# The swapped key copy of the rotary step, moved from VectorE to ScalarE in a two-layer decoder trunk

## The chip, the cores and the metric

The kernel runs on one core of one Trainium2 chip. Its metric is the device time of one execution in microseconds (us). An execution that the hardware profiler took shows what each engine did. The engines are named as the profile names them: PE (TensorE matmuls), PEld (its weight loads), DVE (VectorE), ACT (ScalarE), POOL (GpSimd), SP (the queue that issues the DMAs, SPq in its rows).

## The reference

Two layers of a decoder over 1024 tokens of width 1024. Layer 0 mixes tokens by dilated sliding-window attention in three groups, layer 1 by sliding-window attention with grouped keys and sinks; each mixer is gated, projected, normalised and followed by a gated embedding. The change touches the step between the rotary embedding and the scores.

```python
def apply_rope(t, cos, sin):
    tf = t.astype(jnp.float32)
    half = HEAD_DIM // 2
    t1, t2 = tf[..., :half], tf[..., half:]
    c, s = cos[None, :, None, :], sin[None, :, None, :]
    return jnp.concatenate([t1 * c - t2 * s, t2 * c + t1 * s], axis=-1).astype(t.dtype)
...
def mixer_a(x, w_in, w_out, cos, sin):
    h = x @ w_in
    for gi, (window, dil) in enumerate(A_GROUPS):
        base = 3 * gi * A_WIDTH
        q, k, v = split_cols(h[..., base:base + 3 * A_WIDTH], [A_WIDTH] * 3)
        q = apply_rope(q.reshape(B_, S, A_HEADS, HEAD_DIM), cos, sin)
        k = apply_rope(k.reshape(B_, S, A_HEADS, HEAD_DIM), cos, sin)
        o, lse = banded_attention(strided(q)[:, :, :, None, :], strided(k), strided(v), window // dil)
```

## The kernel before, in words

Every product is made of float16 pieces: a number is split into a high half and a low half (what the high half leaves over), and a product is three matmuls, high by high, high by low, low by high (`lin`, lines 270 to 272; 24 matmuls of 128x512 for a tile of 128 tokens by 512 columns). Tokens stand in 8 tiles of 128.

Layer 0 (`layer_a`, line 622) goes through 2 pairs of head groups, 3 dilations and, in each, a block of values (8 tiles, `v_out`) and two blocks of queries and keys (8 tiles each, 4 query heads and 4 key heads in a tile). So there are 96 query and key tiles. The product of such a tile goes through `rope_out` (line 335): two products with the tables on DVE (lines 345 and 348), their sum on POOL (line 349), the high half on ACT (line 355), the low half on POOL (line 356), the swapped key copy (line 359) and a DMA that transposes the result into `qk` (line 360). A head's row in `hl` is its 64 high halves and then its 64 low halves; the swapped copy of a key has the low halves first, so that two matmuls (line 383) make the full score.

An attention unit is one tile of 4 heads. It runs as `scores` (line 370): the score matmuls on PE (line 383), mask and maximum on DVE (line 387), the bias, four exponentials and the high half of the result on ACT (lines 391, 393, 397), the low half on POOL or DVE (line 399), and a transposing DMA into `pT` (line 402); two units later the value matmuls on PE read `pT` (lines 414 to 416) and ACT copies their result out (line 694). There are 96 units in layer 0 and 32 in layer 1. Score and value matmuls are interleaved with the matmuls of `lin`, and weights of later blocks are prepared meanwhile: maxima on DVE (line 108), a scale over PE (line 235, which waits for line 228 on DVE), and the split on ACT and DVE (lines 131 and 132). At the end of layer 0 the three dilations are merged (`merge`, lines 740 to 768, on DVE, ACT and POOL), and their result is loaded again, transposed to `ogT` and projected.

In layer 1 (`layer_b`, line 787) only the 8 tiles of keys (2 heads, line 805) have the swapped copy; its query tiles have none (`nk` is 0).

What sets the order of the work: each engine has one queue that runs strictly in its order, SP's queue of DMA issues too. The order is not the one of the source: the framework's scheduler arranges the instructions of all engines from its own estimate of their durations (line 1140), so that an instruction put on another engine moves others as well.

Of the kernel before, what the change touches and what calls it, by code (L numbers as in the profile page):

```python
# [14 lines left out]
AF = mybir.ActivationFunctionType  # L15
# [123 lines left out]
class Trunk:  # L139
# [195 lines left out]
    def rope_out(self, ps, nq, nk, n, dst):  # L335

        nc, w = self.nc, self.work
        nh = nq + nk  # L340
        t1 = w.tile([P, 512], F32, tag="t1", name="t1")
        t2 = w.tile([P, 512], F32, tag="t2", name="t2")
        pv = ps.rearrange("p (h c) -> p h c", c=32)
        cos = self.cos[:, n, :].unsqueeze(1).to_broadcast([P, 2 * nh, 32])
        nc.vector.tensor_mul(t1[:, :nh * HD].rearrange("p (h c) -> p h c", c=32), pv, cos)  # L345
        pb = ps.rearrange("p (h b c) -> p h b c", b=2, c=32)[:, :, ::-1, :]
        sin = self.sin[:, n].unsqueeze(1).to_broadcast([P, nh, 2, 32])
        nc.vector.tensor_mul(t2[:, :nh * HD].rearrange("p (h b c) -> p h b c", b=2, c=32), pb, sin)  # L348
        nc.gpsimd.tensor_add(t1[:, :nh * HD], t1[:, :nh * HD], t2[:, :nh * HD])  # L349
        nb = nh + nk  # L350
        hl = w.tile([P, 12, P], F16, tag="hl", name="hl", bufs=3)
        rv = t1[:, :nh * HD].rearrange("p (h c) -> p h c", c=HD)

        def parts():
            nc.scalar.activation(hl[:, :nh, 0:HD], rv, AF.Copy)  # L355
            nc.gpsimd.tensor_sub(hl[:, :nh, HD:P], rv, hl[:, :nh, 0:HD])  # L356
            if nk:
                src, to = (hl[:, a:b, :].rearrange("p h (w c) -> p h w c", w=2) for a, b in ((nq, nh), (nh, nb)))
                nc.vector.tensor_copy(to, src[:, :, ::-1, :])  # L359
            nc.sync.dma_start(dst, hl[:, :nb, :].rearrange("p b c -> p (b c)"), transpose=True)  # L360

        self.ends.append(parts)
# [781 lines left out]
```

## Time and profile before

| | us |
|---|---|
| median of 3 runs | 1685.56 (1683.73 to 1686.35) |
| the profiled execution | 1685.33 |
| its span in the profile | 1683.5 |
| PE busy | 1595.0 (95%) |
| DVE busy | 1130.6 (67%) |
| ACT busy | 871.7 (52%) |
| POOL busy | 677.5 (40%) |

A line of a group gives line, engine, operation, tiles, shape and count, then busy time and the mean duration of one in ns, then the idle time of the engine just ahead of it and what ended it. A line of a timeline gives start and duration in us, and in brackets the idle time ahead with what ended it. In a wait, "A <- B: x, n, y" is x us in all, n times, y the longest.

### The profile page before, as it was taken

To read this page: it belongs to the slowest core of one execution; us is meant where nothing else is said; L and a number is where in the kernel's file an instruction comes from. 1 tells how busy PE (TensorE), PEld (TensorE's weight loads), DVE (VectorE), ACT (ScalarE), POOL (GpSimd) and SP (SyncE) were. 2 spreads that over 40 slices of the span, in tenths; PEclk is the share of its full clock that TensorE was granted. 3 is DMA by queue.
4 is the path that set the end of the run, shared out by engine and by line. 5 is a ranking of instruction groups with operands and counts; after the bars stand their busy time and mean duration, and the time that the engine had idled before them with its cause. 6 is when DMAs were issued, how large, how long until landed. Compare 5 with 4: busy or idle time off the path is not lost. (4 is left out here: it accounts for less than half of the span.)

```text
span 1683.5 us, 29019 instructions
## 1 busy us (share of the span) xinstructions
PE 1595.0 (95%) x10579; PEld 881.5 (52%) x10579; DVE 1130.6 (67%) x2721; ACT 871.7 (52%) x1946; POOL 677.5 (40%) x481
## 2 busy tenths in 40 slices
PE   9898999999999889999999988898999998999999
PEld 3455566654555445766545544344455555544444
DVE  6767556665667776566656696887447898778631
ACT  4525564564755355655647662633232888853321
POOL 0215423532554565234325654443323552225441
PEclk9999999999999999999999999899999999999999
DMA  9617855773678668557647986989965798987963
GB/s 361 242 60 160 171 145 123 174 159 108 140 160 219 190 137 176 151 132 163 155 114 157 193 224 208 316 242 276 233 179 133 139 207 176 182 292 219 248 209 113
DMA packets 543791, 311.02 MB, mean 185 GB/s; under 512 B 473120, under 2 KB 494240, under 8 KB 543392
## 3 DMA queue, kind: packets, MB, share of 16 engines
q1 hardware_dynamic: 543648, 309.16, 74.1%
q8 instruction: 83, 1.36, 0.3%
q14 instruction: 60, 0.49, 0.1%
HBM read 137.78 MB, written 54.92 MB: 114 GB/s over the span
## 5 line engine op out<-in xcount | busy, mean ns | idle before, releaser
L270 PE MATMUL lin<-whl,xhl 128*128 128x512 f16 x1280 | 491.2, 384 | 0.0
L271 PE MATMUL lin<-whl,xhl 128*128 128x512 f16 x1280 | 490.3, 383 | 0.0
L272 PE MATMUL lin<-whl,xhl 128*128 128x512 f16 x1280 | 489.9, 383 | 0.0
L349 POOL TENSOR_TENSOR t<-t,t 128x512 f32<-128x512 f32 (+1 forms) x120 | 152.4, 1270 | 265.2 <-DVE t L348 233.0
L399 POOL TENSOR_TENSOR phl<-sm,phl 128x1024 f16<-128x1024 f32 (+1 forms) x88 | 156.9, 1783 | 245.4 <-ACT phl L397 217.8
L108 DVE TENSOR_REDUCE wpm<-wraw 128x1 f32<-128x1024 f32 (+1 forms) x132 | 157.1, 1198 | 92.6 <-DMA wraw<-in_wa_dram 48.2
L272 PEld LDWEIGHTS <-xhl 128*128 128x128 f16 x1280 | 149.5, 117 | 128.0 <-issue 5.3
L270 PEld LDWEIGHTS <-xhl 128*128 128x128 f16 x1280 | 149.5, 117 | 120.1 <-issue 5.4
L271 PEld LDWEIGHTS <-xhl 128*128 128x128 f16 x1280 | 150.4, 117 | 118.1 <-issue 5.3
L393 ACT ACTIVATE sm<-sm,st,cs 128x128 f32<-128x128 f32 (+1 forms) x384 | 203.6, 532 | 3.8 <-ACT mw L752 0.3
L356 POOL TENSOR_TENSOR hl<-t,hl 128x512 f16<-128x512 f32 (+1 forms) x120 | 145.4, 1212 | 124.6 <-ACT hl L355 124.6
L387 DVE CUSTOM_DVE_ANT_0 sm<-s,tab 128x256 f32<-128x256 f32 (+1 forms) x512 | 156.9, 359 | 33.6 <-PE s L383 31.9
L355 ACT ACTIVATE hl<-t 128x512 f16<-128x512 f32 (+1 forms) x120 | 72.3, 603 | 190.6 <-POOL t L349 181.5
L132 DVE SCALAR_TENSOR_TENSOR whl<-wraw,s,whl 128x1024 f16<-128x1024 f32 (+1 forms) x116 | 161.4, 1445 | 3.1 <-ACT whl L131 3.0
L131 ACT ACTIVATE whl<-wraw,s 128x1024 f16<-128x1024 f32 (+1 forms) x116 | 121.9, 1123 | 26.6 <-PE lin L272 10.2
L270 PE MATMUL lin<-whl,x2T 128*128 128x512 f16 (+1 forms) x320 | 115.5, 361 | 0.0
L271 PE MATMUL lin<-whl,x2T 128*128 128x512 f16 (+1 forms) x320 | 115.2, 360 | 0.0
L272 PE MATMUL lin<-whl,x2T 128*128 128x512 f16 (+1 forms) x320 | 115.2, 360 | 0.0
L397 ACT ACTIVATE phl<-sm 128x1024 f16<-128x1024 f32 (+1 forms) x128 | 110.7, 865 | 3.6 <-DMA pT<-phl 1.6
L345 DVE TENSOR_TENSOR t<-lin,rope 128x512 f32<-128x512 f32 (+1 forms) x120 | 78.9, 658 | 47.2 <-PE lin L272 46.9
L359 DVE COPY hl<-hl 128x512 f16<-128x512 f16 (+1 forms) x104 | 55.7, 535 | 74.7 <-POOL hl L356 74.6
L414 PEld LDWEIGHTS <-pT 128*128 128x128 f16 x800 | 72.8, 99 | 46.4 <-DMA pT<-phl 44.0
(190 smaller groups left out, 2913.7 us busy)
## 6 DMA issues: line engine op xcount, KB each, us to landing
wraw<-in_wa_dram SPq DMA_DIRECT2D x56, 512.0 KB, 5.1
scr<-st SPq DMA_DIRECT2D x96, 132.0 KB, 2.4
gt<-scr SPq DMA_DIRECT2D x48, 264.0 KB, 3.5
wraw<-in_wav_dram SPq DMA_DIRECT2D x24, 512.0 KB, 5.6
prh<-pro SPq DMA_DIRECT2D x32, 256.0 KB, 4.4
wraw<-in_wg_dram SPq DMA_DIRECT2D x16, 512.0 KB, 7.7
wraw<-in_wb_dram SPq DMA_DIRECT2D x16, 512.0 KB, 6.7
xg<-y SPq DMA_DIRECT2D x16, 512.0 KB, 3.8
```

The source lines that it names most:

```text
L108: k.nc.vector.tensor_reduce(pm[:, c:c + 1], self.raw[:, c * q:(c + 1) * q], axis=AX.X, op=ALU.max, apply_absolute_value=True)
L131: nc.scalar.activation(hl[:, 0, sl], self.raw[:, sl], AF.Copy, scale=self.s)
L132: nc.vector.scalar_tensor_tensor(hl[:, 1, sl], self.raw[:, sl], self.s, hl[:, 0, sl], op0=ALU.mult, op1=ALU.subtract)
L270: mm(ps, xh(kt), wh, start=(kt == 0), stop=False)
L271: mm(ps, xh(kt), wl, start=False, stop=False)
L272: mm(ps, xl(kt), wh, start=False, stop=(kt == NK - 1))
L349: nc.gpsimd.tensor_add(t1[:, :nh * HD], t1[:, :nh * HD], t2[:, :nh * HD])
L356: nc.gpsimd.tensor_sub(hl[:, :nh, HD:P], rv, hl[:, :nh, 0:HD])
L387: nc.vector.tensor_tensor_reduce(sm[:, h, :nk], ps[:, i, :nk], mask, 1.0, -3e38, ALU.add, ALU.max, mx[:, h:h + 1])
L393: nc.scalar.activation(sm[:, h, :nk], sm[:, h, :nk], AF.Exp, bias=nbias[:, h:h + 1], scale=cs, accum_out=sums[:, h:h + 1])
L397: nc.scalar.activation(hl[:, 0], sm[:, :, :nk], AF.Copy)
L399: eng.tensor_sub(hl[:, 1], sm[:, :, :nk], hl[:, 0])
```

## The change

The copy is issued on ACT as an activation that copies, with the same source and destination.

```diff
             if nk:
                 src, to = (hl[:, a:b, :].rearrange("p h (w c) -> p h w c", w=2) for a, b in ((nq, nh), (nh, nb)))
-                nc.vector.tensor_copy(to, src[:, :, ::-1, :])
+                nc.scalar.activation(to, src[:, :, ::-1, :], AF.Copy)
             nc.sync.dma_start(dst, hl[:, :nb, :].rearrange("p b c -> p (b c)"), transpose=True)
```

104 copies (96 in layer 0, 8 in layer 1) leave DVE's order and enter ACT's, and the scheduler arranges the rest around them. In ACT's order of the changed kernel 26 of the 96 copies of layer 0 stand directly behind the high half of the same tile (line 355), with nothing between; the others have something between. In 44 of the 96 units of layer 0 a copy stands between the unit's bias (line 391) and its high half (line 397). Three places follow; the names are those of the buffers.

The first is in the first block of queries and keys, about 157 us into the profiled execution: `hl_1366` is the tile whose transpose SP issues just ahead of `pT_1326`. Before, on DVE, and then the change, on ACT:

```order
L387 ISA sm_1406,mx_1407<-s_1415,tab_79 128x128
L387 ISA mx_1407 128x1
L359 COPY hl_1366<-hl_1366 128x512
L399 TENSOR_TENSOR phl_1427<-sm_1406,phl_1427 128x512
L345 TENSOR_TENSOR t1_1491<-lin_1465,rope_650 128x512
```

```order
L355 ACTIVATE hl_1366<-t1_1361 128x8x64
L397 ACTIVATE phl_1323<-sm_1294 128x1024
L694 ACTIVATE st_1108<-o_78,cv17_652 128x256
L359 ACTIVATE hl_1366<-hl_1366 128x512
L391 ACTIVATE st_1405<-mx_1407,ncs22_918 128x4
L694 ACTIVATE st_1199<-o_78,cv17_652 128x256
L393 ACTIVATE sm_1406,st_1405<-sm_1406,st_1405,cs21_915 128x128 x4
L355 ACTIVATE hl_1404<-t1_1399 128x8x64
L397 ACTIVATE phl_1427<-sm_1406 128x512
```

The copy stands behind a unit's copy out (line 694) and ahead of the bias and the exponentials of the next unit.

The second is at the start of a block of values, about 510 us in: `hl_5418` is the last query and key tile of its block, `phl_5449` becomes `pT_5452`. Before, on DVE, and then the change, on ACT:

```order
L359 COPY hl_5374<-hl_5374 128x512
L132 SCALAR_TENSOR_TENSOR whl_5521<-wraw_4455,s56_5383,whl_5521 128x1024 x4
L359 COPY hl_5418<-hl_5418 128x512
L750 TENSOR_REDUCE mM_5508<-gt_5472 128x8
L367 SCALAR_TENSOR_TENSOR vl_649<-lin_5480,vh_648 128x2x256
```

```order
L355 ACTIVATE hl_5418<-t1_5413 128x8x64
L391 ACTIVATE st_5419<-mx_5421,ncs55_4801 128x4
L393 ACTIVATE sm_5420,st_5419<-sm_5420,st_5419,cs54_4798 128x256 x4
L366 ACTIVATE vh_648<-lin_5480 128x2x256
L359 ACTIVATE hl_5418<-hl_5418 128x512
L397 ACTIVATE phl_5449<-sm_5420 128x1024
```

On DVE the copy stood behind four pieces of a weight split; on ACT it stands behind the exponentials of a unit and ahead of that unit's high half.

The third is on DVE alone, at the end of layer 0, about 1029 us in: `gt_11522` is the last merge but one, `whl_11633` the first half of the output projection's weights. Before, and then the change:

```order
L719 SCALAR_TENSOR_TENSOR zu_11561<-zt_11559,zu_11561 128x512
L750 TENSOR_REDUCE mM_11566<-gt_11522 128x8
L751 TENSOR_TENSOR mw_11565<-mM_11566,gt_11522 128x24
L132 SCALAR_TENSOR_TENSOR whl_11633<-wraw_10513,s98_11530,whl_11633 128x1024 x4
L754 TENSOR_TENSOR mwl_11570<-mw_11565,gt_11522 128x24
```

```order
L719 SCALAR_TENSOR_TENSOR zu_11561<-zt_11559,zu_11561 128x512
L132 SCALAR_TENSOR_TENSOR whl_11633<-wraw_10513,s98_11530,whl_11633 128x1024
L766 TENSOR_TENSOR gt_11426<-gt_11426 128x2x256
L132 SCALAR_TENSOR_TENSOR whl_11633<-wraw_10513,s98_11530,whl_11633 128x1024
L750 TENSOR_REDUCE mM_11566<-gt_11522 128x8
L132 SCALAR_TENSOR_TENSOR whl_11633<-wraw_10513,s98_11530,whl_11633 128x1024 x2
L751 TENSOR_TENSOR mw_11565<-mM_11566,gt_11522 128x24
```

The weight split no longer stands behind the merge's first step (line 750), which waits for a load.

## Rows read from the trace of the kernel before

**Rows 1.** The page: its head and busy time of each engine (us, share, instructions).

```profile
span 1683.5 us, 29019 instructions
PE 1595.0 (95%) x10579; PEld 881.5 (52%) x10579; DVE 1130.6 (67%) x2721; ACT 871.7 (52%) x1946; POOL 677.5 (40%) x481
```

**Rows 2.** Busy time by stage: layer 0's attention, then the stretch up to layer 1's.

```profile
core 0: us, PE busy (x) PEld busy (x) DVE busy (x) ACT busy (x) POOL busy (x), PEclk, DMA share, GB/s
118.00:1010.00 892.00, 855.57 (x6163) 508.07 (x6161) 593.93 (x1539) 511.39 (x1286) 411.45 (x297) 0.99 0.70 159
1010.00:1285.00 275.00, 254.24 (x1272) 123.32 (x1273) 182.35 (x361) 99.99 (x134) 105.91 (x79) 0.98 0.84 232
```

**Rows 3.** What PE waited for: 118 to 1010 us, then in the whole span.

```profile
PE o L414 <- DMA pT<-phl: 29.4, 19, 3.8
...
PE s L235 <- DVE mdd L228: 20.3, 4, 7.0
```

**Rows 4.** Groups by line and shape, 118 to 1010 us.

```profile
L356 POOL TENSOR_TENSOR hl<-t,hl 128x512 f16<-128x512 f32 x96 | 120.6, 1256 | 92.8 <-ACT hl L355 92.8
...
L359 DVE COPY hl<-hl 128x512 f16<-128x512 f16 x96 | 53.7, 559 | 71.9 <-POOL hl L356 71.8
...
L397 ACT ACTIVATE phl<-sm 128x512 f16<-128x512 f32 x52 | 32.6, 627 | 1.5 <-DMA pT<-phl 0.3
```

**Rows 5.** The source line of the copy: duration in ns, smallest, median, largest.

```profile
L359 DVE COPY hl<-hl x104: 209/294/2224, 118.3 to 1284.4; 128x512 f16<-128x512 f16 x96, 128x256 f16<-128x256 f16 x8
```

**Rows 6.** Timelines of POOL, DVE, SP and PE, 157 to 168 us.

```profile
157.95 2.14 POOL L399 TENSOR_TENSOR phl<-sm,phl 128x1024 f16<-128x1024 f32 x1
...
158.02 2.21 DVE L359 COPY hl<-hl 128x512 f16<-128x512 f16 x1 [1.72 <-POOL hl L356]
...
160.26 1.44 SPq L360 DMA_TRANSPOSE qk<-hl  x1
161.81 5.03 SPq L402 DMA_TRANSPOSE pT<-phl  x2
...
167.71 0.23 PE L414 MATMUL o<-vh,pT 128*128 128x64 f16 x1 [3.28 <-DMA pT<-phl]
```

**Rows 7.** Timelines of ACT, DVE, SP and PE, 505 to 523 us.

```profile
509.47 0.57 ACT L366 ACTIVATE vh<-lin 128x512 f16<-128x512 f32 x1
...
505.98 5.77 DVE L132 SCALAR_TENSOR_TENSOR whl<-wraw,s,whl 128x1024 f16<-128x1024 f32 x4
511.67 2.22 DVE L359 COPY hl<-hl 128x512 f16<-128x512 f16 x1
...
514.14 1.94 SPq L360 DMA_TRANSPOSE qk<-hl  x1
...
522.43 0.23 PE L414 MATMUL o<-vh,pT 128*128 128x64 f16 x1 [3.48 <-DMA pT<-phl]
```

**Rows 8.** Timelines of ACT, DVE and PE, 608 to 617 us.

```profile
608.34 0.28 ACT L391 ACTIVATE st<-mx,ncs 128x4 f32<-128x4 f32 x1
...
608.41 2.20 DVE L359 COPY hl<-hl 128x512 f16<-128x512 f16 x1 [2.23 <-POOL hl L356]
...
616.38 0.20 PE L414 MATMUL o<-vh,pT 128*128 128x64 f16 x1 [2.86 <-DMA pT<-phl]
```

**Rows 9.** Timelines of POOL, DVE and PE, 580 to 590 us.

```profile
580.33 1.15 POOL L356 TENSOR_TENSOR hl<-t,hl 128x512 f16<-128x512 f32 x1
...
585.28 0.28 DVE L359 COPY hl<-hl 128x512 f16<-128x512 f16 x1
...
589.31 0.62 PE L383 MATMUL s<-qk 128*128 128x128 f16 x8 [3.63 <-DMA qk<-hl]
```

**Rows 10.** Busy time and granted clock (behind POOL) right after those waits; columns as in rows 2.

```profile
167.70:173.40 5.70, 5.69 (x35) 2.92 (x36) 4.54 (x5) 5.63 (x14) 1.35 (x1) 0.50 0.62 134
...
522.40:528.40 6.00, 5.97 (x36) 2.90 (x37) 3.96 (x3) 0.47 (x1) 4.01 (x3) 0.50 0.94 313
...
616.40:620.50 4.10, 4.10 (x33) 1.91 (x34) 1.14 (x5) 2.03 (x5) 2.97 (x2) 0.59 0.71 149
```

**Rows 11.** Timelines of DVE and PE at the end of layer 0.

```profile
1032.59 0.18 DVE L750 TENSOR_REDUCE mM<-gt 128x8 f32<-128x24 f32 x1 [3.10 <-DMA gt<-scr]
...
1051.71 0.29 PE L235 MATMUL s<-mdd,ones 128*128 128x128 bf16 x1 [4.31 <-DVE mdd L228]
...
1077.30 0.29 PE L235 MATMUL s<-mdd,ones 128*128 128x128 bf16 x1 [7.00 <-DVE mdd L228]
```

## The prediction, made before the changed kernel ran

> **What bounds the kernel now.** I read the busy times first: PE is busy for 1595.0 of 1683.5 us [rows 1], so no other engine's busy time sets the end by itself. What a change off PE can move is PE's idle time and the stretches in which its clock is low. So I then read the stages: the attention of layer 0, where 96 of the 104 copies lie, lasts 892 us and leaves PE idle for 36.4 of them (892 less 855.57) at a mean granted clock of 0.99, and DVE is busy there for 593.93 us, ACT for 511.39 [rows 2]. Next the waits: of those 36.4 us PE waits 29.4 us, in 19 waits, for the transposed weights of the attention, `pT` [rows 3]. That is the work to look at: a DMA that SP issues in its own order, behind the transposes of `qk`, and a `qk` transpose may only be issued once the swapped copy of its tile is written. The copy thus holds SP's queue, and `pT` behind it.
>
> The copy itself is uneven. On DVE it takes 294 ns in the median and up to 2224 ns [rows 5], with a mean of 559 ns, and DVE stood idle for 71.9 us ahead of copies, for POOL's low half [rows 4]. The long ones lie beside POOL's work: one starts 0.07 us after POOL's L399 and ends 0.14 us after it [rows 6].
>
> **The change part by part.** *The copies' own time.* DVE is rid of 53.7 us of copies and of 71.9 us of idle time ahead of them [rows 4], 1.31 us a copy. ACT takes 96 copies. No row shows this copy on ACT; the nearest is L397 with the same 512 elements into float16, 627 ns [rows 4], so I take 0.63 us, 60 us in all. Below it lies DVE's 0.29, above it DVE's 2.2 if POOL hindered ACT as it hinders DVE [rows 5]; L397 is nearest, since its engine and its size are the same. ACT goes from 511 to about 571 of 892 us [rows 2], so it is still not full. The 8 small copies of layer 1 and DVE's freed busy time cost or give nothing by themselves, as PE covers both.
>
> *Where the copy held `pT` or `qk`.* Four places show it.
>
> First, 167.7 us. The copy ran from 158.02 to 160.23, SP issued `qk` at 160.26 and `pT` behind it at 161.81, and PE waited 3.28 us [rows 6]. In ACT's new order the copy stands behind a copy out that is then through; with 0.63 us from 158.02 it ends 1.58 us earlier. Gain 1.6.
>
> Second, 522.4 us. The copy stood behind four pieces of weight split that ended at 511.75, and ended itself at 513.89; PE waited 3.48 us later on [rows 7]. On ACT it stands behind L366, which ended at 510.04, so it ends at 510.67, 3.2 us earlier. SP has loads to issue there first, so the gain lies between 0 and 3.2. I take 2.0: PE's order also puts this unit's value matmuls eight matmuls of 128x512 further down, which leaves less to wait for.
>
> Third, 616.4 us. The copy ran from 608.41 to 610.61; behind L391 on ACT, which ended at 608.62, it ends at 609.25 [rows 8]. Gain 1.3 of the wait of 2.86.
>
> Fourth, 589.3 us. POOL was through with the low half at 581.48, but DVE came to the copy only at 585.28, and PE waited 3.63 us for `qk` [rows 9]. On ACT the copy would end near 582.1, some 3.4 us earlier. But the next tiles hang on DVE's own queue, and PE would catch up with them; the gain lies between 0 and 3.4, and I take half, 1.7.
>
> *The clock.* After the first three of these waits PE ran at half its clock (0.50, the 1.2 GHz level, for 5.70 and 6.00 us) or partly so (0.59 over 4.10 us) [rows 10]. That cost 2.85, 3.0 and 1.7 us, 7.5 in all. A mean clock of 0.99 over 892 us [rows 2] leaves some 9 us for all such losses of the stage, so the other waits, shorter on the mean (1.5 us, 29.4 over 19 [rows 3]), hardly lower it. Waits cut to about half should therefore keep the clock; I take the 7.5 as gained, with 0 as the other end.
>
> *The end of layer 0.* DVE stood idle for 3.10 us, for a load of the merge, with the weight split queued behind [rows 11]; in the new order the split comes first. What follows from it (loads of the next weights, their maxima, L228, the last merge) moves up by as much. PE's wait of 4.31 us for L228 shrinks, but the 7.00 us at 1077.3 [rows 11] are then mostly a wait for `ogT`, which hangs on the last merge. So I count what the merge gains, 3.1, between 0 and 4.3.
>
> *What ACT's queue loses.* The copy now stands in the queue that makes `pT`. In 44 of 96 units it sits between bias and high half, and delays that `pT` by 0.63 us; in 26 of 96 tiles it stands directly behind its L355, so ACT must sit through POOL's low half, 1.26 us [rows 4], with the next unit's work behind it. If the 19 waits [rows 3] meet these shares: 19 x 44/96 x 0.63 is 5.5, and 19 x 26/96 x 1.26 is 6.5, together 12.0. Against that, L387 on DVE, the first step of the same chain, no longer queues behind copies at 1.31 us each. I put a third of the loss back, 4.0, leaving 8.0; the ends are 0 and 12.
>
> **The sum.** 1.6 + 2.0 + 1.3 + 1.7 are 6.6, with the clock 14.1, with the end of layer 0 17.2; less 8.0 it is 9.2. The profiled execution took 1685.33 us, so 1676.1; I write 1676. The median of the runs is 1685.56, 0.23 above the execution that the sum stands on. About 0.2%, 3.4 us, is what a measurement can tell from no change.
>
> **The rivals.** *ACT becomes the late engine (slower).* The copies wait for POOL at the head of ACT's queue, and nearly every `pT` that PE already waits for comes later. Then none of the places gains: the chain there was ACT's all along. Price: the 12.0 us above, 1697; with half of that back from DVE 1691, and with two more half-clock stretches at about 3 us each, as in [rows 10], 1703. For it: 26 copies directly behind their L355, 44 in the middle of a unit. Against it: ACT's idle time, 381 us in the stage (892 less 511.39) [rows 2]. It decides once ACT's wait for POOL exceeds the 1.31 us that DVE spends on a copy today. The Trainium skill (ScalarE: Activation LUTs, Rules for kernel authors) speaks on this side: for adds, maxima and the like it says to use VectorE, up to about three times faster per element in bf16 for one source. By that rule the copies are on the wrong engine now, and the time goes up. The trace agrees on copies that run undisturbed and contradicts it for the mean.
>
> As a mechanism of this kernel that reads: 0.63 less 0.29 us, times 96, are 33 us of engine time more; at ACT's share of the stage (511.39 of 892, [rows 2]) 19 us of them would meet a busy ACT. That is 1704 at worst, the far end of this rival. I give it 0.21.
>
> *The gain is larger.* DVE's relief shows on the whole chain and all four places and the layer's end give their upper ends: 1.6 + 3.2 + 1.3 + 3.4 + 4.3 + 7.5 are 21.3, with little lost on ACT: 1664, down to 1655. For it: DVE is the busier of the two in that stage [rows 2], and its copies are stretched most where PE stalls. Chance 0.17.
>
> *Nothing comes of it.* SP's issues and the DMA engines set when `pT` lands: an issue of two transposes took 5.03 us in the first place [rows 6], and the DMA engines are busy for 0.70 of the stage [rows 2]. A copy that ends earlier then only waits in SP's queue. What ACT loses and the clock gives cancel: 1685. Chance 0.20.
>
> **How the numbers follow.** The forecast, 4 to 14 us faster, has 0.42, the larger gain 0.17, no difference 0.20, slower 0.21. Faster by over 0.2% is the first two with one point more from the edge of "nothing", 0.60; within 0.2% is 0.19; slower 0.21. The range runs from 1660, which leaves out the lower half of the larger gain, to 1692, which takes in the near edge of the slower case and leaves out most of it. The cases of gain alone would give 1660 to 1682.
>
> **What would show each step.** The copy on ACT near 0.63 us with little spread; SP's `qk` and `pT` issues of the first and third place over a microsecond earlier against the matmuls around them; PE's waits for `pT` in layer 0 below 29.4 us and fewer half-clock stretches; DVE without 3 us of idle time ahead of the weight split at the layer's end. ACT's idle time ahead of L359, by POOL's low half, shows the loss: some 33 us (26 x 1.26) would be as I count it. Above about 70 us, ACT waits as long as DVE did, and the forecast falls. It is wrong too if PE's waits for `pT` grow in number beyond 19 while the copies end earlier: then ACT's part of the chain decides, not the copy.

## The result, and the profile after the change

The changed kernel took 1675.49 us (median of 6 runs, 1672.76 to 1677.16), the kernel before, in the same job, 1686.30. The ratio is 0.9936, with a 95% interval of 0.9925 to 0.9947: faster by 0.64%, some 10.8 us. The forecast was 1676. The profiled execution of the changed kernel took 1672.76 us, with a span of 1670.9.

The page's head and the two stretches of [rows 1, 2], of the changed kernel:

```profile
span 1670.9 us, 29003 instructions
PE 1587.2 (95%) x10579; PEld 879.7 (53%) x10579; DVE 1080.0 (65%) x2617; ACT 922.0 (55%) x2050; POOL 671.6 (40%) x481
```

```profile
118.00:1010.00 892.00, 866.12 (x6274) 515.00 (x6273) 546.87 (x1466) 562.59 (x1391) 417.31 (x303) 1.00 0.70 162
1010.00:1285.00 275.00, 246.94 (x1206) 119.24 (x1205) 185.01 (x337) 99.99 (x135) 98.70 (x77) 0.95 0.83 229
```

In layer 0's attention PE is busy 10.6 us more of the same 892 us, and the mean clock is 1.00 where it was 0.99. In the stretch behind it PE has lost 7 us, and the clock fell from 0.98 to 0.95. The stretches are the same in time and not quite in work, since the changed kernel is ahead by then. With the leads below they say that the change gains in the attention and gives part of it back at the layer's end. The copies by line and shape from 118 to 1010 us, the source line of all of them (durations in ns: smallest, median, largest), and PE's waits from 118 to 1010 us, to be held against [rows 3 to 5]:

```profile
L359 ACT ACTIVATE hl<-hl 128x512 f16<-128x512 f16 x96 | 59.8, 623 | 55.2 <-POOL hl L356 55.0
```

```profile
L359 ACT ACTIVATE hl<-hl x104: 416/620/633, 118.7 to 1273.7; 128x512 f16<-128x512 f16 x96, 128x256 f16<-128x256 f16 x8
```

```profile
PE o L414 <- DMA pT<-phl: 18.6, 14, 2.8
PE s L383 <- DMA qk<-hl: 6.6, 4, 2.1
```

On ScalarE the copy has no spread to speak of, where VectorE's ran from 209 to 2224 ns. ScalarE sits idle for 55.2 us ahead of the copies, for GpSimd's low halves, as VectorE did for 71.9. The waits for `pT` fell from 29.4 us in 19 to 18.6 in 14.

The timelines of POOL, ACT and SP at the first place of the prediction, to be held against [rows 6]:

```profile
154.10 1.17 POOL L356 TENSOR_TENSOR hl<-t,hl 128x512 f16<-128x512 f32 x1 [1.57 <-ACT hl L355]
155.23 2.14 POOL L399 TENSOR_TENSOR phl<-sm,phl 128x1024 f16<-128x1024 f32 x1
...
155.31 0.63 ACT L359 ACTIVATE hl<-hl 128x512 f16<-128x512 f16 x1
...
155.96 1.44 SPq L360 DMA_TRANSPOSE qk<-hl  x1
...
157.50 2.05 SPq L402 DMA_TRANSPOSE pT<-phl  x1
```

`qk` is issued at 155.96 where it was 160.26, with PE at the same point of its work (within 0.2 us). Of these 4.30 us the copy itself, 0.63 us long in place of 2.21, gives 1.58. The other 2.72 us are older than the copy: GpSimd's L399, which starts as the low half ends, began at 155.23 where it was 157.95. PE's wait of 3.28 us is gone, and so is the half clock behind it (1.00, the 2.4 GHz level, below; 0.50, the 1.2 GHz level, in [rows 10]); a new wait of 2.79 us stands at 225 us. Busy time and granted clock of these two stretches in the changed kernel:

```profile
167.00:174.00 7.00, 7.00 (x50) 4.06 (x49) 4.24 (x12) 6.61 (x18) 5.37 (x4) 1.00 0.41 114
222.00:229.00 7.00, 4.21 (x24) 1.86 (x22) 4.01 (x15) 2.72 (x11) 0.56 (x1) 0.78 0.85 189
```

**Where the time went.** For each projection tile on PE I took the start of its first matmul (L270), before less after, each counted from its profile's first DMA packet. This lead in us, over the profiled execution of the kernel before, is given for the changed kernel and for the experiments told below:

```
start before   changed   e3     e4     e9     e1     e11    e13
   154.4        -0.2     0.2   -0.3    1.1   -1.1   -0.3    0.4
   186.5         7.5     7.8    2.8    6.3    3.2    4.4    8.0
   502.1         8.5     8.5    2.0   10.7   -6.2   -4.2    2.3
   559.5         9.9    10.2    2.5   13.1   -5.1   -5.1    2.8
   623.9        17.7    12.7    6.5   22.0    1.2   -2.2    7.4
  1042.1        19.9    12.0    6.9   25.7  -10.9   -6.4    4.0
  1171.2         8.6     9.5   -2.6   19.9  -13.5  -11.5   -1.2
  1676.6        12.5    12.5   -2.4   22.7  -10.5   -9.9    2.0
```

One profile is worth some us only. Up to 559 us e4 has the order of instructions of the kernel before on every engine, and still a lead of up to 4.1 (2.5 at the end); e12 (below) has the changed kernel's order up to some 1010 us, and at 1008.5 us a lead of 13.1 where that has 18.8. The profiled execution of e9 was 9 us faster than the median of its runs, that of the changed kernel 2.7. So the medians of the runs carry the verdicts, and the leads only say where to look.

### The profile page after: what moved, and what is told of

The parts are those of the page before. It is cut to its first block, busy times and chain, and to the rows that moved or that the text cites. A ratio compares the mean times of both kernels' runs of the same rounds, so it can differ in the third digit from the quotient of the medians.

```text
span 1670.9 us, 29003 instructions
## 1 busy us (share of the span) xinstructions
PE 1587.2 (95%) x10579; PEld 879.7 (53%) x10579; DVE 1080.0 (65%) x2617; ACT 922.0 (55%) x2050; POOL 671.6 (40%) x481
## 4 chain that ended last, share of the span: by engine, by line
PE 59%; DVE 14%; DMA 12%; issue 5%; POOL 4%; ACT 3%; SPq 2%; POOLq 0%; DVEq 0%; ACTq 0%
PE lin L270 18%; PE lin L272 18%; PE lin L271 18%; DMA pT<-phl 4%; DVE whl L132 3%; PE s L383 3%; DVE wpm L108 2%; DMA gt<-scr 2%; ACT sm L393 1%; DVE sm L387 1%; PE o L414 1%; PE o L416 1%; PE o L415 1%; POOL hl L356 1%; DMA wraw<-in_wg_dram 1%
## 5 line engine op out<-in xcount | busy, mean ns | idle before, releaser
L270 PE MATMUL lin<-whl,xhl 128*128 128x512 f16 x1280 | 488.9, 382 | 0.0
L399 POOL TENSOR_TENSOR phl<-sm,phl 128x1024 f16<-128x1024 f32 (+1 forms) x88 | 156.5, 1778 | 259.6 <-ACT phl L397 215.7
L270 PEld LDWEIGHTS <-xhl 128*128 128x128 f16 x1280 | 149.2, 117 | 117.4 <-issue 2.6
L108 DVE TENSOR_REDUCE wpm<-wraw 128x1 f32<-128x1024 f32 (+1 forms) x132 | 157.2, 1198 | 82.7 <-DMA wraw<-in_wa_dram 47.4
L387 DVE CUSTOM_DVE_ANT_0 sm<-s,tab 128x256 f32<-128x256 f32 (+1 forms) x512 | 157.0, 359 | 53.7 <-PE s L383 51.9
L132 DVE SCALAR_TENSOR_TENSOR whl<-wraw,s,whl 128x1024 f16<-128x1024 f32 (+1 forms) x116 | 165.0, 1473 | 4.7 <-ACT whl L131 4.6
L345 DVE TENSOR_TENSOR t<-lin,rope 128x512 f32<-128x512 f32 (+1 forms) x120 | 78.9, 658 | 119.3 <-PE lin L272 83.1
L270 PE MATMUL lin<-whl,x2T 128*128 128x512 f16 (+1 forms) x320 | 114.9, 359 | 0.0
L359 ACT ACTIVATE hl<-hl 128x512 f16<-128x512 f16 (+1 forms) x104 | 63.1, 607 | 59.0 <-POOL hl L356 58.8
```

The source lines that it names most:

```text
L108: k.nc.vector.tensor_reduce(pm[:, c:c + 1], self.raw[:, c * q:(c + 1) * q], axis=AX.X, op=ALU.max, apply_absolute_value=True)
L132: nc.vector.scalar_tensor_tensor(hl[:, 1, sl], self.raw[:, sl], self.s, hl[:, 0, sl], op0=ALU.mult, op1=ALU.subtract)
L270: mm(ps, xh(kt), wh, start=(kt == 0), stop=False)
L387: nc.vector.tensor_tensor_reduce(sm[:, h, :nk], ps[:, i, :nk], mask, 1.0, -3e38, ALU.add, ALU.max, mx[:, h:h + 1])
L399: eng.tensor_sub(hl[:, 1], sm[:, :, :nk], hl[:, 0])
```

## The experiments

My theory was that of the prediction: the copy on VectorE came late and held SyncE's queue, and `pT` behind it. Against it stood that the copy's load on VectorE or its place in VectorE's queue was what cost, that GpSimd ran better, or that the scheduler's new order was lucky. The changed kernel and the 12 experiments, medians in us, each ratio to the kernel before on the same chip:

```
kernel                               keys copied by   median   ratio  95% interval
changed kernel                       ScalarE          1675.5   0.9936 0.9925 to 0.9947
e3 first_pair                        ScalarE / VectorE 1673.8  0.9945 0.9928 to 0.9963
e4 second_pair                       VectorE / ScalarE 1686.4  1.0010 0.9997 to 1.0023
p_before_w15                         VectorE          1685.0   1.0006 0.9993 to 1.0020
p_after_w15                          ScalarE          1677.6   0.9962 0.9947 to 0.9977
e1 VectorE copies too                ScalarE          1696.2   1.0070 1.0052 to 1.0088
e2 ScalarE copies too                VectorE          1687.5   1.0016 0.9998 to 1.0033
e9 ScalarE copies twice              ScalarE          1671.8   0.9915 0.9892 to 0.9938
e10 VectorE copies a table           ScalarE          1679.2   0.9973 0.9962 to 0.9985
e11 VectorE copies 4 elements        ScalarE          1696.0   1.0068 1.0048 to 1.0088
e13 VectorE's maximum of 4 elements  ScalarE          1684.0   0.9988 0.9977 to 0.9998
e8 nothing copied                    (made twice)     1681.6   0.9980 0.9965 to 0.9996
e12 maxima later                     ScalarE          1677.4   0.9962 0.9946 to 0.9978
```

Four missed every range that was expected of them: e1 and e4 came out slower, e3 and e9 faster.

**One half of the change alone: e3 and e4.** `self.pair` is 0 or 1 in layer 0 and 2 in layer 1; e3 takes ScalarE for 0, e4 for 1.

```diff
-                nc.scalar.activation(to, src[:, :, ::-1, :], AF.Copy)
+                if pair == 0:
+                    nc.scalar.activation(to, src[:, :, ::-1, :], AF.Copy)
+                else:
+                    nc.vector.tensor_copy(to, src[:, :, ::-1, :])
```

> ScalarE copies only in the first pair of layer 0 (48 of the 104 copies), VectorE elsewhere. Theory: the lead over the kernel before grows in the first half of layer 0's attention as it did in the changed kernel (by 8 to 15 us at some 560 us), stays there, and in part is given back at the layer's end: 1677 to 1683 us. Rival A (VectorE's load): a gain in the share of the copies, about 5 us: 1680 to 1682 us, spread evenly over that half. Rival B (luck of the order): the lead grows and falls in the second half too, where the code is that of before.

> ScalarE copies only in the second pair of layer 0 (48 of the 104 copies), VectorE elsewhere. Theory: no lead until some 560 us, then 5 to 12 us more by the end of layer 0's attention, of which the layer's end may take back a part: 1677 to 1684 us. Rival A: 1680 to 1682 us, spread evenly. Rival B (luck of the order): a lead or a loss of several us before 560 us, where the code is that of before, or a sum of the two halves' gains that is far from the whole's 10.8 us.

Measured: e3 0.9945, the whole gain; e4 1.0010, none. The first pair's lead repeats (10.2 at 559.5 us, the order there being the changed kernel's). In e4's profile the second pair gains some 4 us (2.5 to 6.9), no more than two profiles of one order differ by, and 9.4 us are lost by 1171 us. What this says: the copies of the first pair carry the result; that those of the second gain something that the layer's end takes away is not shown. Nor does the gain go by the copies that GpSimd holds up, of which more below: e3 and e4 each keep 12 of the 24 long copies of the kernel before, 11 us over the usual length in e3 and 14 in e4.

**Luck of the order: one pair with another number.** The same edit in both kernels:

```diff
-W_STEPS = 1.6
+W_STEPS = 1.5
```

> The kernel before with one number changed that has nothing to do with the copy: weights are prepared by 1.5 steps per tile in place of 1.6, which moves instructions on every engine from the first units on. It is one half of a pair with the changed kernel under the same number. Any cause that lies in the copy itself (late transfer, VectorE's wait, VectorE's load): this one 1680 to 1695 us, and the one with the copy on ScalarE faster by 0.3 to 1.0%. Luck of the order: the difference of the pair lies anywhere from 0.6% slower to 0.6% faster, and need not have the sign of the change.

> The changed kernel with weights prepared by 1.5 steps per tile in place of 1.6, the other half of the pair. A cause in the copy itself: 1670 to 1685 us, 0.3 to 1.0% under its other half. Luck of the order: no more than chance ties it to its other half; a difference below 0.2% or of the other sign speaks for luck.

Measured: 1.0006 and 0.9962, the change again faster, by 0.44%. The sign held in a second pair of orders, and the size moved by 0.2% with it.

**Late transfer or VectorE: e1, e2 and e9.** e1 and e2 add an idle copy of the same elements into `t2`, a work tile that is dead by then, and no transfer reads it. e1, on top of the change:

```diff
                 nc.scalar.activation(to, src[:, :, ::-1, :], AF.Copy)
+                dm = t2.bitcast(F16)[:, :nk * P].rearrange("p (h w c) -> p h w c", w=2, c=HD)
+                nc.vector.tensor_copy(dm, src[:, :, ::-1, :])
```

> ScalarE makes the swapped keys as in the changed kernel, and VectorE copies the same elements once more, behind the same wait for GpSimd, into a dead work tile that no transfer reads. VectorE's load and its waits are thus those of the kernel before; only the transposing transfer of the keys no longer waits for VectorE. Theory (the transfer came late and held SyncE's queue): 1674 to 1680 us, the time of the changed kernel. Rival A (VectorE's load is what cost): 1684 to 1690 us. Rival B (the new order of the work made by luck what was gained): no forecast of the time, but the lead over the kernel before should then grow at other places than in the changed kernel. Rival C (GpSimd disturbed less by VectorE): 1684 to 1688 us, with GpSimd's low halves back near a mean of 1212 ns.

e2, on top of the kernel before:

```diff
                 nc.vector.tensor_copy(to, src[:, :, ::-1, :])
+                dm = t2.bitcast(F16)[:, :nk * P].rearrange("p (h w c) -> p h w c", w=2, c=HD)
+                nc.scalar.activation(dm, src[:, :, ::-1, :], AF.Copy)
```

> VectorE makes the swapped keys as in the kernel before, and ScalarE copies the same elements once more into a dead work tile that no transfer reads: ScalarE carries what it carries in the changed kernel (some 63 us more), and nothing is gained. Theory: 1685 to 1692 us, at least the time before; what lies above 1686 is the price of ScalarE's load and of its wait for GpSimd. Rival A: the same. Rival B (luck of the order): may come out faster than before by as much as the change, below 1682 us.

e9, on top of the change:

```diff
                 nc.scalar.activation(to, src[:, :, ::-1, :], AF.Copy)
+                nc.scalar.activation(to, src[:, :, ::-1, :], AF.Copy)
```

> ScalarE makes the swapped copy twice: the keys' transfer starts some 0.6 us later, more than the 0.43 us by which the copy's mean end after GpSimd's low halves moved between the two kernels, and ScalarE carries 63 us more; VectorE neither waits nor copies. VectorE's wait as the cause: 1675 to 1680 us. The late transfer as the cause: 1682 to 1690 us, the changed kernel's gain gone. If ScalarE's load has a price, up to 8 us more in either case.

Measured: e1 1.0070, e2 1.0016, e9 0.9915. My theory fell with e1 and e9. In e1 the keys' transfer waits for ScalarE alone, as in the changed kernel, and the time is some 22 us worse than that kernel's (1.0070 to 0.9936): VectorE has its copies and their wait back, and the order moved with them. In e9 the transfer starts later than in the kernel before, and nothing is lost. From the end of GpSimd's low half to SP's issue of `qk` the 96 tiles of layer 0 took 2.00 us in the mean in the kernel before, 1.80 in the changed one, 1.89 in e1 and 2.99 in e9: the change itself made the transfer only 0.2 us earlier. The line of e1's idle copies and the page of e9:

```profile
L361 DVE COPY t<-hl 128x512 f16<-128x512 f16 (+1 forms) x104 | 51.2, 492 | 83.1 <-POOL hl L356 83.1
```

```profile
PE 1587.3 (96%) x10579; PEld 880.0 (53%) x10579; DVE 1075.5 (65%) x2617; ACT 972.8 (59%) x2154; POOL 669.1 (40%) x481
```

e9 also settles what ScalarE's load costs: ScalarE is busy 51 us more than in the changed kernel, and the run is not slower (the two intervals meet). e2, where ScalarE also sits idle for 61 us ahead of its copies, agrees: 0.16%, with an interval that takes in zero.

**What on VectorE: load, wait, or being shut out. e10, e11 and e13.** All three stand on the change, and VectorE gets one idle instruction in the place of e1's copy (`dm` as there):

```diff
+                # e10: as many elements, of a constant table
+                nc.vector.tensor_copy(dm, self.tab[:, :nk * 64].bitcast(F16).rearrange("p (h w c) -> p h w c", w=2, c=HD)[:, :, ::-1, :])
+                # e11: 4 elements of the low halves
+                nc.vector.tensor_copy(t2.bitcast(F16)[:, :nk], src[:, :, 1, 0])
+                # e13: the same 4 elements, by a maximum over one element each
+                nc.vector.tensor_reduce(t2[:, :nk], src[:, :, 1, 0:1], axis=AX.X, op=ALU.max)
```

> The changed kernel, and VectorE copies as many elements of a constant table into the dead work tile as it copied in e1: the same load on VectorE, but it waits only for GpSimd's sum, which stands one ScalarE and one GpSimd instruction ahead of the low halves that it waited for in e1 (83 us idle ahead of it there). VectorE's in-order wait as the cause: 1676 to 1684 us, near the changed kernel, with less than 50 us idle ahead of the copies. VectorE's load as the cause: 1690 to 1698 us, as e1. The late transfer as the cause: e1 has spoken against it, and here too it would leave 1674 to 1679 us. Luck of the order: no forecast.

> The changed kernel, and VectorE copies 4 elements of the low halves into the dead work tile, where it copied 512 in e1: the same wait for GpSimd's low halves in VectorE's queue, nearly none of the load (104 times about 0.06 us), and the transfer of the keys not late. VectorE's in-order wait as the cause: 1686 to 1697 us, at or above the time before, as e1. VectorE's load: 1675 to 1680 us. The late transfer: 1674 to 1678 us.

> The kernel of e11 with VectorE's 4-element copy replaced by a 4-element maximum over the same data: the order of the instructions is that of e11 on every engine, and so are the waits, but in the traces so far column maxima on VectorE keep their length beside GpSimd (1.2 us, whatever runs there), while the copies that met a GpSimd instruction lasted to its end (30 of e11's 104, 29 us over their usual 0.17). If being shut out by GpSimd is what costs: 1675 to 1684 us, the gain of the changed kernel back for most of it. If the wait for GpSimd in VectorE's queue costs by itself: 1690 to 1697 us, as e11. In between, the two share it in that proportion. Luck of the order would give the time of e11, since the order is the same.

Measured: e10 0.9973, e11 1.0068, e13 0.9988. e11 has 4 elements where e1 had 512 and costs as much as e1: VectorE's load by elements is not it. The source line of e11's copies and what waited, then the timelines of POOL and DVE at one of them:

```profile
L360 DVE COPY t<-hl x104: 152/170/2091, 118.8 to 1296.4; 128x4 f16<-128x4 f16 x96, 128x2 f16<-128x2 f16 x8
...
  POOL hl L356: 72.7, 39
```

```profile
156.78 1.15 POOL L356 TENSOR_TENSOR hl<-t,hl 128x512 f16<-128x512 f32 x1 [0.74 <-ACT hl L355]
...
157.89 2.14 POOL L400 TENSOR_TENSOR phl<-sm,phl 128x1024 f16<-128x1024 f32 x1
...
157.97 2.09 DVE L360 COPY t<-hl 128x4 f16<-128x4 f16 x1 [3.28 <-POOL hl L356]
...
159.97 0.68 DVE L345 TENSOR_TENSOR t<-lin,rope 128x512 f32<-128x512 f32 x1
```

Four elements take 2.09 us. VectorE first waits 3.28 us for GpSimd's low half. GpSimd goes straight on to its next instruction and is 0.08 us ahead; the copy then ends 0.03 us after that instruction does. Behind it stands L345, the first product of a later tile, which starts only 5.28 us after VectorE fell idle. 30 of the 104 copies are held, by 29 us together, and each of the 30 ends 23 to 31 ns after a GpSimd instruction does. Nine of them had waited for the low half first, as here; the others met a GpSimd instruction without such a wait.

e13 has the order of e11 on every engine, only the form of this one instruction differs. The same views of it:

```profile
L360 DVE TENSOR_REDUCE t<-hl x104: 139/154/165, 118.2 to 1285.8; 128x4 f32<-128x4 f16 x96, 128x2 f32<-128x2 f16 x8
...
  POOL hl L356: 77.8, 39
```

```profile
155.11 2.15 POOL L400 TENSOR_TENSOR phl<-sm,phl 128x1024 f16<-128x1024 f32 x1
...
155.18 0.17 DVE L360 TENSOR_REDUCE t<-hl 128x4 f32<-128x4 f16 x1 [3.73 <-POOL hl L356]
155.26 0.69 DVE L345 TENSOR_TENSOR t<-lin,rope 128x512 f32<-128x512 f32 x1
```

It waits for GpSimd as long (77.8 us, 39 times), but beside the same GpSimd instruction it takes 0.17 us, and L345 starts at once. In e13 too 32 of the 104 start while GpSimd is at work, as many as in e11, and none is held. The ratio of the two, 1.0068 over 0.9988, is 1.0080: being shut out costs e11 some 13.5 us, with the order the same and the waits and the load nearly so. What is left between e13 and the changed kernel, 0.9988 over 0.9936 or 0.5%, some 9 us, goes to the wait in VectorE's queue, to the 16 us that the 104 maxima take themselves, or to the order that changed with them; no run here parts these. e10 waits earlier, for GpSimd's sum (69.7 us idle, not under 50 as I expected), and is shut out 18 times, by 15 us; it lies between.

The Trainium skill (SBUF — State Buffer, Who interferes with whom) says that a VectorE copy of the faster, two-port kind and a GpSimd instruction exclude each other for the whole length of the one that is first, and that a `tensor_reduce` on trn2 never meets this. The traces agree on both: 2.09 us for 4 copied elements beside an instruction of 2.14 us, and at most 0.165 us in 104 maxima. That these copies are of the two-port kind no run shows.

**Two attempts at more: e8 and e12.** In e8 no copy is left; both halves are written a second time into the swapped place:

```diff
-                nc.scalar.activation(to, src[:, :, ::-1, :], AF.Copy)
+                nc.scalar.activation(to[:, :, 1, :], rv[:, nq:nh], AF.Copy)
+                nc.gpsimd.tensor_sub(to[:, :, 0, :], rv[:, nq:nh], to[:, :, 1, :])
```

> Nothing is copied: ScalarE writes the keys' high halves a second time, from the turned products, into the swapped place, and GpSimd subtracts a second time into the other. ScalarE no longer waits for GpSimd's low halves (59 us idle in the changed kernel), its second instruction has 256 elements in place of 512 (about 0.4 us in place of 0.61, some 20 us less), and GpSimd has 104 subtractions of 256 elements more (about 0.7 us each, some 70 us on 672). If ScalarE's wait and load still cost: 1666 to 1674 us. If GpSimd's length now sets when the keys are whole: 1676 to 1686 us, with more waits for keys than the changed kernel's 6.6 us. If neither matters: within 2 us of the changed kernel.

Measured: 0.9980, most of the gain lost. GpSimd's second subtraction is the price, in GpSimd's line of e8:

```profile
L360 POOL TENSOR_TENSOR hl<-t,hl 128x256 f16<-128x256 f32 (+1 forms) x104 | 82.8, 796 | 0.0
```

But the waits for keys hardly grew (7.4 us in 2, from 6.6 in 4). VectorE's L345 waited for this subtraction, 17.3 us in 11 times; how the 83 us reach PE stays open.

e12 looks at the end of layer 0:

```diff
                 self.z_tile(self.work, n, half)
-                self.progress()
+                self.progress(1.2)
```

> The changed kernel with the weights prepared by 1.2 steps per tile in place of 1.6 while the last block of each layer's attention stage (the gate's product) runs: VectorE's four column maxima of a weight block, which stand ahead of the last merge's product in the changed kernel, then stand behind it. If those maxima cost the changed kernel its lead at the end of layer 0: the time from the last value product to the last merge's store falls from 43.8 us to 37 to 40, and the run takes 1667 to 1673 us. If the weights that come later make TensorE wait in their place: 1675 to 1683 us. If the end of the layer is set by something else, no difference: 1673 to 1678 us.

In the changed kernel PE stands still twice there, from the timelines of PE and DVE, with the busy time and the clock (0.76) of that stretch:

```profile
1036.16 0.29 PE L235 MATMUL s<-mdd,ones 128*128 128x128 bf16 x1 [8.75 <-DVE mdd L228]
...
1064.86 0.58 PE L270 MATMUL lin<-whl,ogT 128*128 128x512 f16 x1 [10.23 <-ACT whl L131]
```

```profile
1025.99 1.22 DVE L108 TENSOR_REDUCE wpm<-wraw 128x1 f32<-128x1024 f32 x1 [1.68 <-DMA wraw<-in_wg_dram]
...
1030.83 0.17 DVE L758 TENSOR_TENSOR mw<-mw,mL 128x24 f32<-128x24 f32 x1
...
1036.02 0.68 DVE L766 TENSOR_TENSOR gt<-gt 128x512 f32<-128x512 f32 x1
```

```profile
1028.00:1070.00 42.00, 23.60 (x88) 9.69 (x89) 33.23 (x59) 22.72 (x30) 16.63 (x11) 0.76 0.84 278
```

Three of four maxima (L108, the first behind a wait of 1.68 us for its load) stand ahead of the last merge's L758 on VectorE, where the kernel before had all four behind it. From the last value matmul to the last merge's store took 43.8 us, in the kernel before 38.1, in e3 38.3. e12 brought this to 39.1, as expected, yet the run is 0.9962, no faster than the changed kernel. In its profile the last value matmul itself came 5.1 us later, with the order the same up to there, and layer 1, which the edit touches too, lost: from 1396 to 1555 us its lead fell from 9.2 to 6.2 where the changed kernel's rose to 12.5. So the maxima explain the longer merge; that they cost the run time is not shown.

No kernel here is clearly better than the changed one: e9 and e3 have lower medians or as low, but their intervals meet that of the changed kernel.

## Why the prediction was right, and where its reasons were wrong

The time was right (1676 against 1675.5), and that was luck: two errors of some 14 us cancelled, and the reason ahead of the sum was not the cause.

- **The copies' own time.** Right: 0.623 us in the mean on ScalarE, taken as 0.63, with no stretch beside GpSimd.
- **"The copy thus holds SP's queue, and `pT` behind it."** This is the step that failed as the cause. The transfers did come earlier, by 0.2 us in the mean, but e1 takes VectorE out of the keys' path and gains nothing, and e9 makes them later and loses nothing. What the runs show to cost is an instruction's place in VectorE's queue, with the products and the scores' reductions (L345, L387) behind: shut out by GpSimd (0.8%, e11 against e13), and with it the wait for GpSimd or the order that goes with it (0.5%, e13 against the changed kernel). That the gain of the change itself comes from there is argued from this, not shown by a run. Of this I had only the part that I set under the rival of a larger gain, as VectorE's relief on the whole chain. I had seen the mark of it, a long copy that starts 0.07 us after GpSimd's L399 and ends 0.14 after it, and had read it as a longer copy, not as a held queue.
- **The four places.** Three of the waits are gone or short: at the tile of 167.7 us none above 0.9 us is left, at 522.4 one of 1.05, at 616.4 none above 0.9. The fourth, 3.63 us for `qk`, split into 1.0, 1.65 and 2.14 at the next tiles: PE catches up with VectorE, as I had it. At the first place the 1.6 agrees with the copy's part (1.58); the 2.72 us that came from ahead of the copy I missed.
- **The clock.** 7.5 us were counted. The first place's half clock is gone (1.00), others came (0.78 at 225 us); the stage's mean went from 0.99 to 1.00. The direction is right, the size can't be read more closely.
- **ScalarE's queue, 8.0 lost.** Mis-sized, and by most. ScalarE's idle time ahead of the copies was 55.2 us, not 33, and still neither e9 (51 us more on ScalarE, no slower) nor e2 (0.16%, zero within its interval) finds a price near 8.0. The lead at the end of layer 0's attention was thus 19.9 us, where 14.1 less 8.0 was forecast.
- **The end of layer 0, 3.1 gained.** Wrong in sign. The lead fell from 19.9 to 8.6 between 1042 and 1171 us; the merge's chain came only 13.3 us earlier than before (last store at 1036.9 us for 1050.2) while PE came 19 us earlier, so PE waited and its clock fell. So, by these profiles, the attention came out 13.8 us better than summed and the layer's end 14.4 worse, and the two errors cancelled; layer 1 added 3.9 us that the sum did not have.
- **The rivals.** ScalarE as the late engine fell: e9 doubles its copies. By the rule of the Trainium skill that I cited there (ScalarE: Activation LUTs, Rules for kernel authors), and that I stretched from adds and maxima to copies, they belonged on VectorE; they ran slower on ScalarE (0.62 us against 0.294 undisturbed), and the kernel was faster. I also wrote that the trace contradicts the rule for the mean. It does not: with the disturbed ones the mean on VectorE was 559 ns [rows 4], still under ScalarE's 623. "Nothing comes of it" fell with the interval. The larger gain had the relief of VectorE that the runs point to; in the profile the layer's end took back what it would have added.

Four things are open. How the 10.8 us of the change divide between being shut out, the wait and the new order: the kernel before with its copies in a form that GpSimd doesn't hold was not run. How the last 9 us between e13 and the changed kernel divide. Why e1 and e11 are 12 us slower than the kernel before, which has the same wait and as many held copies (24, by 26 us, to e1's 22, by 21); e2 has both copies, as e1 has, and as many held (23, by 21 us), and is 9 us faster than e1, so order may be worth as much as the change itself. And why the first pair carries the whole gain, when both pairs have as many held copies.

## What to carry to other kernels

When an instruction waits on one engine for another, ask what stands behind it in its own queue before asking who reads its result; an idle instruction of 4 elements with the same wait shows in one run whether such a place costs, though not what moving the real one gains (here some 22 us, e11 against the changed kernel, where the change gained 10.8). A VectorE copy that meets a GpSimd instruction can last until that one ends, as 24 of 104 did here. Of the 43 that had waited for GpSimd, 9 started right behind its next instruction, and all 9 were held. Moving such a copy to ScalarE, or giving it a form that GpSimd doesn't hold, is worth a run. And hold a lead in one stage against the end of the stage: a chain on other engines can take it back.

## What the hardware showed that I had not expected

- A VectorE copy of 4 float16 elements took 2.09 us beside a GpSimd instruction of 2.14 us, and 0.17 us otherwise; a VectorE maximum of the same 4 elements never took more than 0.165 us. With the order of all instructions the same, this form was worth 0.80% between e11 and e13.
- ScalarE's copies, 96 of 512 and 8 of 256 elements, took 416 to 633 ns in the changed kernel whatever ran on GpSimd (399 to 634 in e9), and 104 more of them (e9) cost nothing that could be measured.
